# Low-rank decay columns computed with the first head's values and transposed, and the first weights in slots

## The chip, the core and the metric

The kernel runs on one core of one Trainium2 chip. The core has a matrix engine (PE in the profile, with PEld for its weight loads), three engines for element-wise work (DVE, ACT and POOL), and SP, on whose queue most transfers are issued. Each engine takes its instructions in the order in which the program gives them, and waits on semaphores for what the others have to finish first. The metric is the time of one execution on the device in microseconds (us); the median of several runs counts.

## The reference

One layer of a hybrid encoder on 1024 tokens of 1024 features, in fp32. What matters here is the normalised input, the one projection that feeds everything behind it, and the decay that is made of 32 of its columns:

```python
h = rmsnorm(x, norm_mix[l])
proj = h @ w_in[l]
q, k, v, r, lr_f, lr_b, u, g_a, g_b = jnp.split(proj, split_points, axis=-1)
log_a_f = jax.nn.log_sigmoid((lr_f @ w_decay_up_fwd[l] + b_decay_fwd[l]).astype(jnp.float32)) / GATE_NORMALIZER
log_a_b = jax.nn.log_sigmoid((lr_b @ w_decay_up_bwd[l] + b_decay_bwd[l]).astype(jnp.float32)) / GATE_NORMALIZER
...
```

`lr_f` and `lr_b` have 16 columns each: the low-rank columns. `q` and `k` have 4 heads of 128 columns, `v` 4 heads of 256. Behind it come gated linear attention in both directions, a pooling mixer, their merge, an output projection and a feed-forward network.

## The kernel before

**Numbers.** PE multiplies in fp32r. Each operand is split into a high part (ACT casts it) and a low part (DVE or POOL subtracts the high part from the source; `split_to`, L196 to L198), and a product is three matmuls: high by high, high by low, low by high (`mm3`). Names ending in h and l are such pairs: `hh` and `hl` the normalised input, `wh` and `wl` weights, `vh` and `vl` values.

**The start.** SP's queue carries the first tiles of `x`, six small vectors into `rows` (gains and decay biases; `load_rows`, L353), the first head's V weights in four parts (`fetch`, L243), more tiles of `x`, and `lraw`, the 32 low-rank columns of `w_in` for all features. PE transposes `rows` into `vps`, DVE copies it to `cols`. A tile is 128 tokens. For each, ACT makes the mean square, DVE and POOL the factor `n1rs`, DVE scales to `xn` (`norm_x`); PE transposes `xn` so that features lie on partitions (`tr`); ACT and DVE apply the gain and split it into `hh` and `hl` (`gain_and_split`, L320 to L330).

**The value tiles.** The loop over the eight tiles, numbered 0 to 7, in pairs (L428 to L443) makes the first head's values (`values`, L380): in each tile eight feature blocks by three matmuls, with 128 tokens of `hh` or `hl` stationary and 256 weight columns moving, into one PSUM bank, and then the split into `vh` and `vl`. Beside it runs a generator that `pump` advances after each feature block by credits: in even tiles (until tile 2) the norms of later tiles, in odd tiles up to 5 a block of four transposes after feature blocks 0, 2, 4 and 6, with their `gain_and_split`, for the next two tiles. Each tile's products can start once the features of its pair are split.

**The low-rank stage.** `low_rank_weights` (L396) casts `lraw` to `lw`, with the 32 columns repeated four times, three times the high part and once the low part. After the loop (L445 to L456), for each half of the tokens 16 matmuls with `lw` stationary and 512 tokens of `hh` or `hl` moving give the low-rank columns with features on partitions (128 rows: four copies of 32); `lrT` is their cast, with one group of rows replaced by the residual. Products with `up`, made of the two small decay matrices, use it later, after the projections of Q and K.

**Weights.** The class `Weights` (L213) takes tiles from rings of buffers; their casts and subtractions are steps in `pending`, which `pump` takes up one by one. `fetch` loads the next weights of the list `order`, `prepare` puts their splitting up, `take` waits for it. For the first weights DVE subtracts in part 0 and POOL in parts 1 to 3.

**Order.** The program's order is that of each engine. Eight semaphores are handed round among the DMAs; a DMA that takes one again waits until the transfer that had it before has landed.

Of the kernel before, what the change touches and what calls it, by code (L numbers as in the profile page):

```python
# [10 lines left out]
F32 = mybir.dt.float32  # L11
F32R = mybir.dt.float32r
# [3 lines left out]
ALU = mybir.AluOpType  # L16

P = 128
D = 1024
SEQ = 1024  # L20
KT = D // P
NT = SEQ // P
HALF = 512
HEADS = 4
DK = 128
DV = 256
RANK = 16
# [8 lines left out]
Q0, K0, V0, R0 = 0, 512, 1024, 2048  # L36
LR0 = 3072
U0 = LR0 + 2 * RANK
# [4 lines left out]
AHEAD = 4  # L43
PUT = 3
POOLING = 1.75

SLOTS = 39
MM_BANKS = 3
# [3 lines left out]
def kernel(  # L52
# [20 lines left out]
    nc = tc.nc  # L73
    x, out = x[0], out[0]
    w_in, w_branch, w_out = w_in[0], w_branch_gla[0], w_out[0]
# [4 lines left out]
    wts = ctx.enter_context(tc.tile_pool(name="wts", bufs=6))  # L80
    tmp = ctx.enter_context(tc.tile_pool(name="tmp", bufs=5))
    small = ctx.enter_context(tc.tile_pool(name="small", bufs=5))
    ps_mm = ctx.enter_context(tc.tile_pool(name="ps_mm", bufs=MM_BANKS, space=bass.MemoryType.PSUM))
    ps_g = ctx.enter_context(tc.tile_pool(name="ps_g", bufs=8 - MM_BANKS, space=bass.MemoryType.PSUM))
# [6 lines left out]
    def name(s):  # L91
        count[0] += 1
        return f"{s}_{count[0]}"

    def slot(dtype=F32, shape=(2, HALF), s="slot"):
        return slots.tile([P, *shape], dtype, tag="slot", name=name(s))
# [4 lines left out]
    def s1(shape=(256,), s="s"):  # L101
        return small.tile([P, *shape], F32, tag="s1", name=name(s))
# [4 lines left out]
    def bank(pool, s="ps"):  # L107
        return pool.tile([P, HALF], F32, tag=pool.name, name=name(s))

    def as_f32(ap):  # L110
        return ap.bitcast(F32)


    ident = const.tile([P, P], F32, tag="ident", name="ident")
# [36 lines left out]
    def soon(delay, *steps):  # L151
        put_off.extend([delay, step] for step in steps)
# [5 lines left out]
    def pump(dt):  # L158
        for entry in put_off:
            entry[0] -= dt  # L160
        while put_off and put_off[0][0] <= 0:
            put_off.pop(0)[1]()
        if pending:
            credit[0] += dt
            if credit[0] >= 2:
                credit[0] = 0.0
                pending.pop(0)()
        if aside:
            aside[0][1] -= dt

            if aside[0][1] <= 0 and not pending:
                cost = next(aside[0][0], None)
                if cost is None:
                    aside.pop(0)
                else:
                    aside[0][1] += cost
        if not side:
            return
        side[0][1] -= dt
        while side and side[0][1] <= 0:  # L180
            try:
                side[0][1] += next(side[0][0])
            except StopIteration:
                side.pop(0)

    def begin(gen, delay=0.0):
        side.append([gen, delay])

    def finish_side():
        while side:  # L190
            for _ in side[0][0]:
                pass
            side.pop(0)


    def split_to(hi, lo, src, eng=nc.vector):  # L196
        nc.scalar.copy(hi, src)  # L197
        eng.tensor_tensor(lo, src, as_f32(hi), op=ALU.subtract)  # L198
# [13 lines left out]
    class Weights:  # L212
# [8 lines left out]
        def split(self, raw):  # L221
            hi = wts.tile(list(raw.shape), F32R, tag="wh", name=name("wh"))[:, :, :]
            lo = wts.tile(list(raw.shape), F32R, tag="wl", name=name("wl"))[:, :, :]
            split_to(hi, lo, raw[:, :, :], nc.gpsimd if hT.tiles else nc.vector)
            self.parts.append((hi, lo))

        def finish(self):
# [3 lines left out]
        def __call__(self, k):  # L231
            return tuple(t[:, k % self.per, :] for t in self.parts[k // self.per])


    order = []
    for h in range(HEADS):
        cols_of = [(Q0 + h * DK, DK), (K0 + h * DK, DK), (V0 + h * DV, DV)]
        order += [(w_in, KT, *c) for c in (cols_of if h else cols_of[2:] + cols_of[:2])]
    order += [(w_in, KT, R0 + j * P, P) for j in range(KT)]
    order = iter(order)  # L240
    loaded, ready = [], []

    def fetch():  # L243
        src = next(order, None)
        if src is not None:
            loaded.append(load(*src))

    def prepare():
        if not loaded:
            fetch()  # L250
        if loaded:
            ready.append(Weights(loaded.pop(0)))

            credit[0] = -2.0

    def take(ahead=True):

        if not ready:
            prepare()
        w = ready.pop(0)  # L260
        w.finish()
        if ahead:
            prepare()
        return w
# [3 lines left out]
    def products(ps, a, b, first=True, last=True, onto=False):  # L268

        for n, (i, j) in enumerate(((0, 0), (0, 1), (1, 0))):  # L270
            nc.tensor.matmul(ps, a[i], b[j], start=first and n == 0, stop=last and n == 2, skip_group_check=onto)  # L271

    def mm3(ps, a, b, first, last, onto=False):
        products(ps, a, b, first, last, onto)
        pump(ps.shape[-1] / HALF)
# [15 lines left out]
    def tokens(pair, t):  # L291
        return tuple(p[:, (t % 4) * P : (t % 4 + 1) * P] for p in pair)
# [52 lines left out]
    n_rows = sum(n for _, n in vec_rows)  # L345
    rows = tmp.tile([n_rows, P], F32, tag="t2", name="rows")
    uraw = slot(F32, (HEADS, 2, DK), "uraw")
    lraw = slot(F32, (KT, 2 * RANK), "lraw")

    def load_x(t):  # L350
        nc.sync.dma_start(xt[t % 4][:, :], x[t * P : (t + 1) * P, :])

    def load_rows(at, v, n):  # L353
        nc.sync.dma_start(rows[at : at + n, :], v[0].rearrange("(j p) -> j p", p=P))

    def load_up(i, d, w):
        r = 2 * RANK * i + RANK * d
        nc.sync.dma_start(uraw[r : r + RANK, :, d, :], w[0].rearrange("r (h c) -> r h c", h=HEADS))

    load_x(0)  # L360
    load_rows(0, *vec_rows[0])
    load_x(1)
    for i in range(1, len(vec_rows)):
        load_rows(sum(n for _, n in vec_rows[:i]), *vec_rows[i])
    fetch()
    for t in (2, 3):
        load_x(t)
    nc.sync.dma_start(lraw[:, :, :], w_in[:, LR0:U0].rearrange("(k p) c -> p k c", p=P))
    nc.gpsimd.memset(uraw[:, :, :, :], 0.0)

    hT = Activations("h")
# [12 lines left out]
    def values(w, v, t):  # L384
        ps = bank(ps_mm)
        for kt in range(KT):
            mm3(ps[:, :DV], tokens(hT(kt, t // 4), t), w(kt), kt == 0, kt == KT - 1)
        split_to(*(part[:, t % 4, :] for part in v[t // 4]), ps[:, :DV])
# [1 line left out]

    lw = [wts.tile([P, 4, 4, 2 * RANK], F32R, tag="wh", name=name("lw")) for _ in range(2)]
    up = slot(F32R, (HEADS, 2, DK), "up")

    def low_rank_weights():  # L396
        for i in range(2):
            raw = lraw[:, 4 * i : 4 * i + 4, :]
            nc.scalar.copy(lw[i][:, :, :3, :], raw.unsqueeze(2).broadcast_to([P, 4, 3, 2 * RANK]))
            nc.vector.tensor_tensor(lw[i][:, :, 3, :], raw, as_f32(lw[i][:, :, 0, :]), op=ALU.subtract)  # L400
        nc.scalar.copy(up[:, :, :, :], uraw[:, :, :, :])
        nc.vector.tensor_tensor(up[32:64], uraw[32:64], as_f32(up[32:64]), op=ALU.subtract)

    def value_slots():
        return [(slot(F32R, (4, DV), "vh"), slot(F32R, (4, DV), "vl")) for _ in range(2)]

    v = value_slots()
# [10 lines left out]
    for t in range(2):  # L418
        for kp, ps in enumerate(trs):
            transpose_tile(ps, xn[t], t, kp)  # L420
    prepare()
    for kp, ps in enumerate(trs):
        pending.pop(0)()
        gain_and_split(ps, kp, 0, hT, g_mix)
    w = take(ahead=False)
    norm_x(2)
    norm_x(3)
    for t in range(0, NT, 2):  # L428
        if t + 4 < NT:
            begin(norms(t + 4), 1)  # L430
        if t == 2:
            for d, w_up in enumerate((w_decay_up_fwd, w_decay_up_bwd)):
                for i in range(4):
                    load_up(i, d, w_up)
        values(w, v, t)
        finish_side()
        if t + 2 < NT:
            begin(to_features(xn[(t + 2) % 4 :], t + 2, hT, g_mix), 0.5)
        values(w, v, t + 1)
        finish_side()  # L440
        if t == 4:
            low_rank_weights()
    prepare()  # L443
    lrT = slot(F32R, (2, HALF), "lrT")
    for half in range(2):  # L445
        ps = bank(ps_mm)
        for k in range(KT):
            for i in range(2):
                nc.tensor.matmul(
                    ps[:, :], lw[k // 4][:, k % 4, :, :].rearrange("p a r -> p (a r)"), hT(k, half)[i],  # L450
                    start=k == 0 and i == 0, stop=k == KT - 1 and i == 1,
                )
            pump(2 / 3)
        nc.scalar.copy(lrT[:, half, :], ps[:, :])
        nc.vector.tensor_tensor(lrT[64:96, half, :], ps[64:96, :], as_f32(lrT[64:96, half, :]), op=ALU.subtract)


    deferred = []

    def later(dst, src):  # L460
# [376 lines left out]
    for h in range(HEADS):  # L837
# [4 lines left out]
        if h > 0:  # L842
            v = value_slots()
            w = take()
# [136 lines left out]
    for j in range(KT):  # L981
# [6 lines left out]
        w = take()  # L988
# [7 lines left out]
        for half in range(2):  # L996
            ps = feature_major(w, hT, half)
# [188 lines left out]
    def pooling():  # L1186

        for g in range(GROUPS):
# [7 lines left out]
            for cost in pooled(g, u, hi, lo):  # L1196
                yield POOLING * cost
            yield 4
# [646 lines left out]
```

## Time and profile before

| | |
|---|---|
| median of 3 runs | 1407.31 us (1405.72 to 1408.82) |
| span of the profiled execution | 1405.0 us |
| instructions in the span | 18577 |
| value tiles, first to last matmul on PE | 10.77 to 43.57 us |
| low-rank stage on PE | 43.41 to 50.69 us |

The profile is one execution, recorded by the hardware. The span runs from its first to its last instruction; the device time also holds what lies around it. In rows of the timeline the first number is the start from the beginning of the span, the second the duration, both in us; then come the engine, the line of the program, the operation, what it writes and reads with shapes, how many instructions the row holds and, in brackets, how long the engine was idle before it and who ended that. Matmuls are pipelined: the distance of two starts is what one costs in a stream, and the duration of one is longer. Rows of stages have the length of the stage, the busy time and count for each engine, the clock granted to PE (1.00 is full speed), the DMA share and GB/s.

### The profile page before, as it was taken

To read this page: it belongs to the slowest core of one execution; us is meant where nothing else is said; L and a number is where in the kernel's file an instruction comes from. 1 tells how busy PE (TensorE), PEld (TensorE's weight loads), DVE (VectorE), ACT (ScalarE), POOL (GpSimd) and SP (SyncE) were. 2 spreads that over 40 slices of the span, in tenths; PEclk is the share of its full clock that TensorE was granted. 3 is DMA by queue.
4 is the path that set the end of the run, shared out by engine and by line. 5 is a ranking of instruction groups with operands and counts; after the bars stand their busy time and mean duration, and the time that the engine had idled before them with its cause. 6 is when DMAs were issued, how large, how long until landed. Compare 5 with 4: busy or idle time off the path is not lost.

```text
span 1405.0 us, 18577 instructions
## 1 busy us (share of the span) xinstructions
PE 1372.1 (98%) x6677; PEld 1155.0 (82%) x6677; DVE 842.7 (60%) x1073; ACT 623.5 (44%) x1119; POOL 751.0 (53%) x558
## 2 busy tenths in 40 slices
PE   7999999999999989999999999999999999999997
PEld 6889898988888768788887788888888888888876
DVE  6266757567745666677885865555655556343363
ACT  6364655554333444455356633333333334443253
POOL 3251616141288446567666076667666667464354
PEclk9999999999999999999999999999999999999999
DMA  6212413322377558998524555554444447976451
GB/s 192 76 46 61 135 52 114 98 69 75 121 214 250 195 173 273 334 406 291 185 75 151 186 188 173 173 167 148 140 146 148 140 155 255 387 259 222 165 227 72
DMA packets 167612, 243.62 MB, mean 173 GB/s; under 512 B 10936, under 2 KB 98016, under 8 KB 167520
## 3 DMA queue, kind: packets, MB, share of 16 engines
q1 hardware_dynamic: 167520, 242.45, 51.0%
q8 instruction: 52, 0.85, 0.2%
q14 instruction: 40, 0.33, 0.1%
HBM read 164.55 MB, written 77.86 MB: 173 GB/s over the span
## 4 chain that ended last, share of the span: by engine, by line
PE 67%; DVE 5%; issue 3%; DMA 2%; POOL 2%; ACT 2%; SPq 0%; POOLq 0%; ACTq 0%; DVEq 0%
PE ps L271 64%; DMA fraw<-in_w_in_dram 1%; POOL wl L198 1%; PE yb L271 1%; PE tp L959 0%; DMA gor<-g_out 0%; DMA wor<-t_out 0%; DVE fs L869 0%; PE op L800 0%; DVE ws L1033 0%; POOL fraw L600 0%; DVE x L1523 0%; POOL mg L1150 0%; DMA u_out<-uph 0%; ACT wh L197 0%
## 5 line engine op out<-in xcount | busy, mean ns | idle before, releaser
L198 POOL TENSOR_TENSOR wl<-fs,wh 128x512 fp32r<-128x512 f32 x120 | 166.1, 1388 | 172.1 <-ACT wh L197 138.6
L271 PE MATMUL ps<-gl,wh 128*128 128x512 f32 x616 | 239.8, 389 | 0.9 <-DVE gl L1439 0.9
L271 PE MATMUL ps<-gh,wh 128*128 128x512 f32 x616 | 240.3, 390 | 0.0
L271 PE MATMUL ps<-gh,wl 128*128 128x512 f32 x616 | 239.7, 389 | 0.0
L198 POOL TENSOR_TENSOR wl<-fraw,wh 128x512 fp32r<-128x512 f32 x90 | 128.9, 1432 | 60.1 <-ACT wh L197 57.3
L198 POOL TENSOR_TENSOR ol<-gor,oh 128x1024 fp32r<-128x1024 f32 (+1 forms) x42 | 100.1, 2389 | 93.2 <-ACT oh L197 87.5
L271 PE MATMUL ps<-hh,wh 128*128 128x512 f32 x376 | 149.6, 398 | 0.0
L271 PE MATMUL ps<-hh,wl 128*128 128x512 f32 x376 | 147.0, 391 | 0.0
L271 PE MATMUL ps<-hl,wh 128*128 128x512 f32 x376 | 146.7, 390 | 0.0
L198 POOL TENSOR_TENSOR wl<-raw,wh 128x512 fp32r<-128x512 f32 x47 | 64.5, 1389 | 146.6 <-ACT wh L197 135.7
L271 PEld LDWEIGHTS ps<-gl,wh 128*128 128x128 f32 x616 | 115.6, 188 | 25.0 <-DVE gl L1439 1.3
L271 PEld LDWEIGHTS ps<-gh,wl 128*128 128x128 f32 x616 | 115.6, 188 | 23.9
L271 PEld LDWEIGHTS ps<-gh,wh 128*128 128x128 f32 x616 | 115.6, 188 | 23.9
L271 PE MATMUL ps<-oh,oh 128*128 128x512 f32 x308 | 119.9, 389 | 1.1 <-DVE x L1767 1.1
L271 PE MATMUL ps<-ol,oh 128*128 128x512 f32 x308 | 119.9, 389 | 0.2 <-DVE ol L198 0.2
L271 PE MATMUL ps<-oh,ol 128*128 128x512 f32 x308 | 119.8, 389 | 0.0
L198 POOL TENSOR_TENSOR wl<-wraw,wh 128x512 fp32r<-128x512 f32 x56 | 89.8, 1631 | 45.1 <-ACT wh L197 45.0
L198 DVE TENSOR_TENSOR ol<-wor,oh 128x1024 fp32r<-128x1024 f32 (+1 forms) x42 | 62.0, 1496 | 54.0 <-ACT oh L197 46.7
L197 ACT CAST wh<-fs 128x512 fp32r<-128x512 f32 x120 | 73.7, 614 | 29.0 <-DVE fs L869 27.8
L271 PEld LDWEIGHTS ps<-hh,wl 128*128 128x128 f32 x376 | 70.7, 188 | 15.1
L271 PEld LDWEIGHTS ps<-hl,wh 128*128 128x128 f32 x376 | 70.9, 188 | 13.6
L271 PEld LDWEIGHTS ps<-hh,wh 128*128 128x128 f32 x376 | 70.8, 188 | 13.5
(251 smaller groups left out, 3183.0 us busy)
## 6 DMA issues: line engine op xcount, KB each, us to landing
fraw<-in_w_ffn_in_dram SPq DMA_DIRECT2D x44, 512.0 KB, 5.9
gor<-g_out SPq DMA_DIRECT2D x35, 512.0 KB, 6.1
raw<-in_w_in_dram SPq DMA_DIRECT2D x48, 256.0 KB, 3.2
g_out<-s SPq DMA_DIRECT2D x44, 256.0 KB, 2.3
fraw<-in_w_in_dram SPq DMA_DIRECT2D x20, 512.0 KB, 6.8
wor<-t_out SPq DMA_DIRECT2D x20, 512.0 KB
g_out<-g SPq DMA_DIRECT2D x33, 256.0 KB, 2.6
x<-in_x_dram SPq DMA_DIRECT2D x16, 512.0 KB, 5.7
```

The costliest lines, as they stand in the source:

```text
L197: nc.scalar.copy(hi, src)
L198: eng.tensor_tensor(lo, src, as_f32(hi), op=ALU.subtract)
L271: nc.tensor.matmul(ps, a[i], b[j], start=first and n == 0, stop=last and n == 2, skip_group_check=onto)
```

## The change

The 32 low-rank columns of `w_in` stand behind the 256 columns of the first head's V weights in the same tiles, so that a value matmul has 288 moving columns (`VL`). In the bank of each value tile, columns 256 to 287 then hold the low-rank columns with tokens on partitions. ACT copies them, repeated four times, to `lr` (128 x 128); PE transposes `lr` into the bank `lt`, in the next tile's matmuls after feature block 1, and for tile 7 within Q's first ones. After four of them ACT casts the bank to `lrT` and DVE makes the residual rows. The low-rank stage, `lw` and `lraw` go.

The first weights have slots of their own. Their narrow columns are loaded on ACT's queue ahead of all else, their wide ones on SP's. The split goes to DVE in parts 0 and 2 and to POOL in parts 1 and 3. Three instead of four copies of each decay matrix are loaded to `uraw`. Q's weights are fetched in the loop and put up for splitting within it.

```diff
+VL = DV + 2 * RANK
...
-            split_to(hi, lo, raw[:, :, :], nc.gpsimd if hT.tiles else nc.vector)
+            split_to(hi, lo, raw[:, :, :], nc.gpsimd)
...
+    class FirstWeights(Weights):
+        def split(self, raw):
+            hi, lo = (slot(F32R, (2, VL), s) for s in ("fwh", "fwl"))
+            split_to(hi[:, :, :], lo[:, :, :], raw[:, :, :], nc.gpsimd if len(self.parts) % 2 else nc.vector)
+            self.parts.append((hi, lo))
+
+    def load_first():
+        tiles = [slot(F32, (2, VL), "fraw") for _ in range(KT // 2)]
+        for i, t in enumerate(tiles):
+            rows_in = slice(2 * i * P, (2 * i + 2) * P)
+            nc.scalar.dma_start(t[:, :, DV:], w_in[rows_in, LR0:U0].rearrange("(k p) c -> p k c", p=P))
+        return tiles
+
+    def load_first_values(tiles):
+        for i, t in enumerate(tiles):
+            rows_in = slice(2 * i * P, (2 * i + 2) * P)
+            nc.sync.dma_start(t[:, :, :DV], w_in[rows_in, V0 : V0 + DV].rearrange("(k p) c -> p k c", p=P))
...
-        order += [(w_in, KT, *c) for c in (cols_of if h else cols_of[2:] + cols_of[:2])]
+        order += [(w_in, KT, *c) for c in (cols_of if h else cols_of[:2])]
...
+    first_raw = load_first()
     load_x(0)
...
-    fetch()
+    load_first_values(first_raw)
     for t in (2, 3):
         load_x(t)
-    nc.sync.dma_start(lraw[:, :, :], w_in[:, LR0:U0].rearrange("(k p) c -> p k c", p=P))
...
+    def up_weights():
         nc.scalar.copy(up[:, :, :, :], uraw[:, :, :, :])
         nc.vector.tensor_tensor(up[32:64], uraw[32:64], as_f32(up[32:64]), op=ALU.subtract)
+
+    low_rows, low_banks = {}, {}
+
+    def first_values(w, v, t):
+        ps = bank(ps_mm)
+        for kt in range(KT):
+            mm3(ps[:, :VL], tokens(hT(kt, t // 4), t), w(kt), kt == 0, kt == KT - 1)
+            if kt == 1 and t - 1 in low_rows:
+                transpose_low(t - 1)
+        split_to(*(part[:, t % 4, :] for part in v[t // 4]), ps[:, :DV])
+        low_rows[t] = s1((4, 2 * RANK), "lr")
+        nc.scalar.copy(low_rows[t][:, :, :], ps[:, DV:VL].unsqueeze(1).broadcast_to([P, 4, 2 * RANK]))
+
+    def transpose_low(t):
+        half, i = t // 4, t % 4
+        if i == 0:
+            low_banks[half] = bank(ps_g, "lt")
+        ps = low_banks[half]
+        nc.tensor.transpose(
+            ps[:, i * P : (i + 1) * P], low_rows.pop(t).rearrange("p a r -> p (a r)"), ident[:, :]
+        )
+        if i == 3:
+            nc.scalar.copy(lrT[:, half, :], ps[:, :])
+            nc.vector.tensor_tensor(lrT[64:96, half, :], ps[64:96, :], as_f32(lrT[64:96, half, :]), op=ALU.subtract)
...
-    prepare()
+    w = FirstWeights(first_raw)
...
-                for i in range(4):
+                for i in range(3):
                     load_up(i, d, w_up)
-        values(w, v, t)
+        first_values(w, v, t)
...
-        values(w, v, t + 1)
+        first_values(w, v, t + 1)
         finish_side()
+        if t == 2:
+            fetch()
         if t == 4:
-            low_rank_weights()
-    prepare()
-    lrT = slot(F32R, (2, HALF), "lrT")
-    for half in range(2):
-        ps = bank(ps_mm)
-        for k in range(KT):
-            for i in range(2):
-                nc.tensor.matmul(
-                    ps[:, :], lw[k // 4][:, k % 4, :, :].rearrange("p a r -> p (a r)"), hT(k, half)[i],
-                    start=k == 0 and i == 0, stop=k == KT - 1 and i == 1,
-                )
-            pump(2 / 3)
...
+            up_weights()
+            prepare()
+    soon(1, partial(transpose_low, NT - 1))
```

The next rows are ACT's order around the end of value tile 0, before and then with the change. `ps_256` and `ps_257` are the bank of tile 0, `tr_299` and `tr_302` the first block of transposes for tiles 2 and 3; the names in brackets are the engines whose semaphores are waited for.

```order
L311 ACTIVATE xn_131,n1ms_281<-x_127 128x1024 [waits DMAHW0_49,DVE_49]
L197 CAST vh_160<-ps_256 128x256 [waits PE_49]
L325 ACTIVATE hh_206<-tr_299,cols 128x256 [waits PE_49]
L325 ACTIVATE hh_206<-tr_299,cols 128x256
L325 ACTIVATE hh_216<-tr_314,cols 128x256 [waits PE_49]
```

```order
L331 ACTIVATE xn_131,n1ms_282<-x_127 128x1024 [waits DMAHW3_49,DVE_49]
L198 CAST vh_161<-ps_257 128x256 [waits PE_49]
L430 COPY lr_296<-ps_257 128x128 [waits DVE_49]
L345 ACTIVATE hh_207<-tr_302,cols 128x256 [waits PE_49]
L345 ACTIVATE hh_207<-tr_302,cols 128x256
L345 ACTIVATE hh_217<-tr_319,cols 128x256 [waits PE_49]
```

A copy to `lr` now stands between the cast of the values and the casts of the features, and it waits for DVE: for the count that DVE reaches with `vl` of the same tile.

On PE the rows are those of tile 1 with the change, from the end of the block of transposes that follows its feature block 0 to the start of feature block 2. `ps_298` is the bank of tile 1, `lt_314` the bank for the transposed low-rank columns.

```order
L338 MATMUL tr_302<-ident,xn_133 128x128 [waits DVE_49]
L338 MATMUL tr_302<-ident,xn_133 128x128
L291 MATMUL ps_298<-fwh_203,hh_207 128x288
L291 MATMUL ps_298<-fwl_204,hh_207 128x288
L291 MATMUL ps_298<-fwh_203,hl_208 128x288
L438 MATMUL lt_314<-ident,lr_296 128x128 [waits PE_49,Activation_49]
L291 MATMUL ps_298<-fwh_213,hh_217 128x288
```

The transpose of tile 0's copy stands within tile 1 and waits for ACT.

On SP the rows are the first loads of the program, before and then with the change.

```order
L351 DMA x_127<-in_x_dram 128x1024
L354 DMA rows<-in_norm_ffn_dram 8x128
L354 DMA rows<-in_gla_norm_dram 8x128
L354 DMA rows<-in_pool_scale_dram 8x128
L354 DMA rows<-in_b_decay_fwd_dram 4x128
L354 DMA rows<-in_b_decay_bwd_dram 4x128
L205 DMA raw_145<-in_w_in_dram 128x2x256 [waits DMAHW0_49]
```

```order
L370 DMA x_127<-in_x_dram 128x1024
L373 DMA rows<-in_norm_ffn_dram 8x128
L373 DMA rows<-in_gla_norm_dram 8x128 [waits DMAHW0_49]
L373 DMA rows<-in_pool_scale_dram 8x128 [waits DMAHW1_49]
L373 DMA rows<-in_b_decay_fwd_dram 4x128 [waits DMAHW2_49]
L373 DMA rows<-in_b_decay_bwd_dram 4x128 [waits DMAHW3_49]
L253 DMA fraw_136<-in_w_in_dram 128x2x256 [waits DMAHW4_49]
```

The four narrow loads on ACT's queue hold the first four semaphores, so the last four loads of `rows` wait for them to land.

More of the change, by code (lines that the diff above doesn't have):

```diff
@@ L347 @@
     uraw = slot(F32, (HEADS, 2, DK), "uraw")
-    lraw = slot(F32, (KT, 2 * RANK), "lraw")
     def load_x(t):
@@ L388, in values @@
         split_to(*(part[:, t % 4, :] for part in v[t // 4]), ps[:, :DV])
-    lw = [wts.tile([P, 4, 4, 2 * RANK], F32R, tag="wh", name=name("lw")) for _ in range(2)]
     up = slot(F32R, (HEADS, 2, DK), "up")
-    def low_rank_weights():
-        for i in range(2):
-            raw = lraw[:, 4 * i : 4 * i + 4, :]
-            nc.scalar.copy(lw[i][:, :, :3, :], raw.unsqueeze(2).broadcast_to([P, 4, 3, 2 * RANK]))
-            nc.vector.tensor_tensor(lw[i][:, :, 3, :], raw, as_f32(lw[i][:, :, 0, :]), op=ALU.subtract)
+    lrT = slot(F32R, (2, HALF), "lrT")
+    def up_weights():
         nc.scalar.copy(up[:, :, :, :], uraw[:, :, :, :])
         nc.vector.tensor_tensor(up[32:64], uraw[32:64], as_f32(up[32:64]), op=ALU.subtract)
+    low_rows, low_banks = {}, {}
[19 more added lines that the diff above has]
+            nc.vector.tensor_tensor(lrT[64:96, half, :], ps[64:96, :], as_f32(lrT[64:96, half, :]), op=ALU.subtract)
     def value_slots():
@@ L424 @@
         gain_and_split(ps, kp, 0, hT, g_mix)
-    w = take(ahead=False)
+    w.finish()
     norm_x(2)
@@ L438 @@
             begin(to_features(xn[(t + 2) % 4 :], t + 2, hT, g_mix), 0.5)
-        values(w, v, t + 1)
+        first_values(w, v, t + 1)
         finish_side()
+        if t == 2:
+            fetch()
         if t == 4:
-            low_rank_weights()
-    prepare()
-    lrT = slot(F32R, (2, HALF), "lrT")
-    for half in range(2):
-        ps = bank(ps_mm)
-        for k in range(KT):
-            for i in range(2):
-                nc.tensor.matmul(
-                    ps[:, :], lw[k // 4][:, k % 4, :, :].rearrange("p a r -> p (a r)"), hT(k, half)[i],
-                    start=k == 0 and i == 0, stop=k == KT - 1 and i == 1,
-                )
-            pump(2 / 3)
-        nc.scalar.copy(lrT[:, half, :], ps[:, :])
-        nc.vector.tensor_tensor(lrT[64:96, half, :], ps[64:96, :], as_f32(lrT[64:96, half, :]), op=ALU.subtract)
+            up_weights()
+            prepare()
+    soon(1, partial(transpose_low, NT - 1))
     deferred = []
```

## The prediction

> **What bounds the kernel now.** I read the page from the top: the span, the busy times, and the chain of work that ended last.
>
> ```profile
> span 1405.0 us, 18577 instructions
> PE 1372.1 (98%) x6677; PEld 1155.0 (82%) x6677; DVE 842.7 (60%) x1073; ACT 623.5 (44%) x1119; POOL 751.0 (53%) x558
> PE 67%; DVE 5%; issue 3%; DMA 2%; POOL 2%; ACT 2%; SPq 0%; POOLq 0%; ACTq 0%; DVEq 0%
> ```
>
> PE is busy for 98% of the span and carries the chain. An instruction taken from PE is therefore time won where PE has no idle time, and a wait put into PE's stream is time lost there. So I asked for busy time by stage. The columns are the stage, its length, the busy time of PE, weight load, DVE, ACT and POOL, then the granted clock.
>
> ```profile
> 0.00:75.00 75.00, 65.19 (x397) 58.11 (x398) 30.79 (x71) 36.72 (x77) 18.94 (x54) 1.00 0.42 125
> 29.50:43.00 13.50, 13.50 (x117) 13.50 (x116) 9.02 (x22) 7.46 (x18) 0.00 (x0) 1.00 0.07 19
> ```
>
> The change lies within the first 75 us. There PE is idle for 9.8 us, nearly all of it before 29.5, and from 29.5 to 43, the later value tiles, it is idle for nothing: there is no slack in that stretch to hide a new wait. Behind the change the order on every engine is as before, so what the first 50 us win or lose is handed on to the end by a busy PE.
>
> **Removed: the low-rank stage.** The timeline of PE at its two ends:
>
> ```profile
> 43.29 0.28 PE L271 MATMUL ps<-wh,hl 128*128 128x256 f32 x1
> 43.41 0.40 PE L449 MATMUL ps<-hh,lw 128*128 128x512 f32 x1
> ...
> 50.69 0.39 PE L271 MATMUL ps<-hh,wh 128*128 128x512 f32 x1
> ```
>
> 32 matmuls start from 43.41 on and the first projection of Q starts at 50.69, 0.2275 each without a gap: **-7.28 us**, all of it on the path.
>
> **Added: 32 columns.** Eight tiles of 24 matmuls are 192. From 43.29 to 43.41 a matmul of 256 columns takes 0.12 us, one of 512 takes 0.2275. The slope is 0.1075 us per 256 columns, 0.0134 for 32, so that one takes 0.133: 192 x 0.0134 = **+2.58 us**.
>
> **Added: eight transposes on PE.** No single one stands in a stream of matmuls before, but blocks of four do:
>
> ```profile
> 33.30 0.29 PE L271 MATMUL ps<-wh,hl 128*128 128x256 f32 x1
> 33.43 0.60 PE L318 MATMUL tr<-ident,xn 128*128 128x128 f32 x4
> 33.78 0.36 PE L271 MATMUL ps<-wh,hh 128*128 128x256 f32 x1
> 33.98 0.28 PE L271 MATMUL ps<-wl,hh 128*128 128x256 f32 x1
> ```
>
> From 33.30 to 33.98 pass 0.68 us where two matmuls alone take 0.24: a block costs 0.44. Of this the four need 0.35 (33.43 to 33.78), 0.088 each, and the rest, 0.08, is the slower matmul behind them. One alone costs 0.17: 8 x 0.17 = **+1.36 us**. Up to here the sum is -3.34.
>
> **Added: the wait at each transpose.** PE takes its work in order, so the transpose of tile t, which stands behind the second feature block of tile t+1, holds everything behind it until ACT's copy `lr` of tile t is there. And by the built program this copy waits for DVE's `vl` of the same tile: the two read the same PSUM bank and are put in sequence. So the chain behind a value tile is: ACT's `vh`, DVE's `vl`, ACT's `lr`, PE. ACT takes work in order too: behind the waiting copy are the casts of `hh` and the squares for the norms. The copy itself is not in the trace; casts on ACT take 0.37 us at 256 columns and 0.62 at 512 (rows below), about 0.98 ns per column, so I take 0.25 for 128; at the 0.37 of 256 columns all eight waits below would grow by 0.12, 1.0 in all, and at the 0.19 of DVE's copy of 40 columns (a row further down) shrink by 0.5. Between dependent engines pass about 0.04 us (43.57, where the last matmul ends, to 43.61 here):
>
> ```profile
> 43.61 0.37 ACT L197 CAST vh<-ps 128x256 fp32r<-128x256 f32 x1 [2.51 <-PE ps L271]
> 43.88 0.62 ACT L197 CAST wh<-raw 128x512 fp32r<-128x512 f32 x1
> 44.01 0.42 DVE L198 TENSOR_TENSOR vl<-ps,vh 128x256 fp32r<-128x256 f32 x1 [1.94 <-ACT vh L197]
> ```
>
> This is the chain with both engines idle: `vl` ends at 44.43, the copy at 44.72, the transpose may start at 44.76. With six matmuls of 0.133 from 43.41 PE would be there at 44.21: **0.55** late, the stall in tile 7. At Q three wide matmuls (0.68) come first: 44.09, so **0.65**. In tile 5 a block of transposes (0.44) comes first too: **0.1**.
>
> Where DVE is busy it is later. In tiles 2, 4 and 6 the casts of the transposes of the tile before stand ahead of `vl`; the rows are those of tile 6:
>
> ```profile
> 36.87 0.60 PE L318 MATMUL tr<-ident,xn 128*128 128x128 f32 x4
> 37.22 0.36 PE L271 MATMUL ps<-wh,hh 128*128 128x256 f32 x1
> 38.23 0.37 ACT L197 CAST vh<-ps 128x256 fp32r<-128x256 f32 x1
> 38.38 0.88 DVE L328 SCALAR_TENSOR_TENSOR hl<-tr,cols,hh 128x256 fp32r<-128x256 f32 x2 [0.27 <-ACT hh L325]
> 39.17 0.41 DVE L198 TENSOR_TENSOR vl<-ps,vh 128x256 fp32r<-128x256 f32 x1
> ```
>
> `vl` ends at 39.58, the transpose may start at 39.91; PE is there nine matmuls after 37.22, at 38.5: 1.4 late, three times **4.2**.
>
> In tile 1 DVE holds two norms ahead of `vl`:
>
> ```profile
> 18.64 0.44 PE L318 MATMUL tr<-ident,xn 128*128 128x128 f32 x2 [1.04 <-DVE n1rs L302]
> 18.83 0.36 PE L271 MATMUL ps<-wh,hh 128*128 128x256 f32 x1
> 19.37 0.35 ACT L197 CAST vh<-ps 128x256 fp32r<-128x256 f32 x1
> 21.45 0.42 DVE L198 TENSOR_TENSOR vl<-ps,vh 128x256 fp32r<-128x256 f32 x1
> ```
>
> `vl` ends at 21.87, the transpose may start at 22.2; PE is there at 19.3, three matmuls after 18.83: **2.9**. In tile 3 the norms of tile 2 stand ahead:
>
> ```profile
> 23.55 1.08 ACT L311 ACTIVATE xn<-x 128x1024 f32<-128x1024 f32 x1
> 25.25 0.14 DVE L302 TENSOR_SCALAR n1rs<-n1ms 128x1 f32<-128x1 f32 x1
> 28.34 0.42 DVE L198 TENSOR_TENSOR vl<-ps,vh 128x256 fp32r<-128x256 f32 x1
> ```
>
> Counted from the end of the copy that freed tile 2: the square takes 1.2 with its read-out, the chain from `n1rs` to the end of `vl` 3.5 (25.25 to 28.76), the copy 0.3, together 5.0. PE needs 18 matmuls (2.4), six more (0.8), a block and a transpose: 3.85. Late by **1.15**. All waits: 0.55 + 0.65 + 0.1 + 4.2 + 2.9 + 1.15 = **+9.55 us**. The low bound is 2.25: had the copy to wait for `vh` alone, tile 1 would be 0.75 late, tiles 2, 4, 6 0.4 each, the last two 0.3.
>
> The Trainium skill, "PSUM — Partial Sum Buffer", section "PSUM bank collisions raise a hardware error", states that two engines on one bank and quadrant at once are an error, reads against reads included; it speaks against a change that gives a bank a second reader on another engine. By that rule the sum is the one with 9.55 and not the one with 2.25; no run here shows a collision.
>
> **Moved: the start.** Four narrow loads (128-byte runs) now go out on ACT's queue first, and eight semaphores are handed round, so the last four loads of `rows` on SP each wait for a narrow load to land.
>
> ```profile
> 0.80 0.39 SPq L351 DMA_DIRECT2D x<-in_x_dram  x1
> 3.44 0.29 SPq L354 DMA_DIRECT2D rows<-in_b_decay_bwd_dram  x1
> 6.71 0.30 PE L411 MATMUL vps<-ident,rows 40*128 40x40 f32 x1 [6.71 <-DMA rows<-in_b_decay_bwd_dram]
> 7.13 0.19 DVE L413 COPY cols<-vps 128x40 f32<-128x40 f32 x1
> 7.52 0.15 DVE L302 TENSOR_SCALAR n1rs<-n1ms 128x1 f32<-128x1 f32 x1 [0.20 <-ACT xn L311]
> DMA to landing us min/median/max: 2.1/2.7/3.3
> DMA to landing us min/median/max: 2.8/3.1/3.7
> ```
>
> The last two are the landings of `uraw` (16 partitions) and `raw` (256 KB). Issues 0.4 apart put the fourth at 2.0; at `uraw`'s 2.7 it lands at 4.7, and the last `rows` goes out then, not at 3.44: 1.26 later. DVE's copy of the columns has 0.2 to spare ahead of the second tile's `n1rs`, which starts the next tile's way to PE: 1.0 late. With landings of 2.1 and 3.7 it is 0.4 and 2.1; I take 1.0, near `uraw`, the smaller load, and bounds of 0 and 2.1. Three wider casts of the first weights on ACT add 0.06 each: **+1.2 us**.
>
> **At nothing.** The first weights' residual moves from POOL to DVE for one of four:
>
> ```profile
> PE ps L271 <- POOL wl L198: 1.0, 3, 0.5
> ```
>
> PE waits 1.0 for POOL there, but ahead of the norms for which it waits 1.04 at 18.64 anyhow. The earlier fetch and casts of Q's weights lie under tiles 3 to 7, and ACT is busy for 7.46 of 13.5 us there. The casts of `lrT` are needed by the decay products only after Q's and K's projections. Without that cover they would cost about one cast each, 0.6.
>
> **Sum.** -7.28 + 2.58 + 1.36 + 9.55 + 1.2 = **+7.4 us**: from the profiled span of 1405.0 to 1412.4, and from the median of 1407.31, which holds 2.3 us around the span, to **1414.7**.
>
> **The rivals.** B, half clock. After an idle of 2.27 us PE ran slow later in the program:
>
> ```profile
> 514.72 0.50 PE L271 MATMUL ps<-trh,wh 128*128 128x512 f32 x1 [2.27 <-DVE ga L1237]
> 515.00:520.00 5.00, 5.00 (x16) 3.95 (x16) 4.90 (x6) 2.28 (x5) 3.05 (x2) 0.66 0.00 0
> 517.15 0.63 PE L271 MATMUL ps<-trh,wl 128*128 128x512 f32 x1
> 517.58 0.63 PE L271 MATMUL ps<-trh,wh 128*128 128x512 f32 x1
> ```
>
> The granted clock is 0.66 over 515 to 520, and matmuls start 0.43 apart: 5 x 0.34 = 1.7 us lost. The stall of 2.9 in tile 1 is longer, with 1.04 of idle just ahead of it at 18.64. Once gives 1416.4, twice 1418.1. Against it: one idle is one case. The Trainium skill, "TensorE: Matmul & The Clock Gate", section "Part 1: The HAM clock gate", puts the throttle behind an idle window of about 3.4 us; by that rule 2.9 would cost nothing more, but the trace shows half clock after 2.27, and the measurement decides.
>
> C, the copy does not wait for `vl` on the chip, or DVE gets there earlier than its rows say: stalls of 2.25, so -3.34 + 2.25 + 1.2 = +0.1, 1407.4. The order of waits in the built program speaks against it.
>
> D, faster: the copy of each tile lands within the 0.8 us that PE needs for six matmuls, and the start does not move. Then -3.34 stands alone, 1404.0; it decides as soon as stalls and start together stay under 0.5. Against it, `vh`, `vl` and copy are 1.04 even with idle engines.
>
> **Chances.** The forecast 0.55 (1413.2 to 1416.8 with the bounds of the start and of the copy), B 0.27, C 0.10, D 0.04, several costs beyond these 0.04. Within 0.2%, 2.8 us, is about what a measurement of this kernel can tell from no change: 1404.5 to 1410.1. So faster 0.05, same 0.09, slower 0.86. The range takes in the forecast and B: 1410.5 to 1419.5.
>
> **What would show it.** PE from the last value tile straight to Q, with no 512-column low-rank matmuls; value matmuls 0.133 apart; in PE's waits eight at the new transpose, for ACT's copy, near 2.9, 1.4, 1.15, 1.4, 0.1, 1.4, 0.55 and 0.65, and on ACT the copy idle for DVE's `vl`; the start of the columns' copy near 8.4 instead of 7.13; a clock under 1.00 around 22 to 26 for B. I am wrong if the copies run right behind `vh`, or if the stalls move what comes later.

## The result and the profile after

The changed kernel takes 1415.17 us (median of 4 runs, 1414.63 to 1417.15), the kernel before beside it 1407.18. The medians are 8.0 us apart, where +7.4 was forecast. The ratio over all runs, which need not be the quotient of the medians, is 1.0062 (95% interval 1.0050 to 1.0075): slower. Measured a second time (experiment 5), the medians were 10.5 us apart and the ratio 1.0070 (1.0057 to 1.0082).

The page of the changed kernel, in the rows that answer to those of before: span, busy times, and shares of the chain that ended last.

```profile
span 1415.4 us, 18528 instructions
PE 1372.9 (97%) x6653; PEld 1154.9 (82%) x6653; DVE 844.6 (60%) x1072; ACT 624.8 (44%) x1125; POOL 750.0 (53%) x557
PE 60%; DVE 6%; issue 4%; POOL 4%; DMA 3%; ACT 2%; SPq 0%; POOLq 0%; DVEq 0%; ACTq 0%
```

The span is 10.4 us longer than before, and PE is busy for 0.8 us more: the loss is idle time of PE. This profiled execution is the slowest of the four, which matters below. What PE waited for up to 80 us, with the sum, the count and the longest:

```profile
PE vps L452 <- DMA rows<-in_b_decay_bwd_dram: 8.6, 1, 8.6
PE lt L438 <- ACT lr L430: 8.4, 7, 2.7
PE tr L338 <- DVE n1rs L322: 1.6, 2, 1.0
PE ps L291 <- POOL fwl L199: 1.1, 2, 0.6
```

The second row is new: the eight transposes, seven of them waiting for ACT's copy. Who holds the copy is seen on ACT and DVE in tile 1, and what it does to PE on PE's own timeline:

```profile
20.43 0.35 ACT L198 CAST vh<-ps 128x256 fp32r<-128x256 f32 x1
23.60 0.27 ACT L430 COPY lr<-ps 128x128 f32<-128x128 f32 x1 [2.82 <-DVE vl L199]
23.15 0.42 DVE L199 TENSOR_TENSOR vl<-ps,vh 128x256 fp32r<-128x256 f32 x1
20.88 0.29 PE L291 MATMUL ps<-fwh,hl 128*128 128x288 f32 x1
23.92 0.48 PE L438 MATMUL lt<-ident,lr 128*128 128x128 f32 x1 [2.75 <-ACT lr L430]
```

The copy is done as soon as `vl` is, and not sooner, 3.2 us after the cast of the same bank began. PE could have gone on at 20.88 + 0.133 = 21.01 and did so at 23.92: 2.91. The profile calls 2.75 of this idle, because a matmul's row lasts longer than its share of the stream; by distances of starts each wait is 0.16 longer than its idle time. The other waits, and the matmuls around the one in tile 2:

```profile
30.13 0.30 PE L291 MATMUL ps<-fwl,hh 128*128 128x288 f32 x1
...
30.92 0.29 PE L291 MATMUL ps<-fwl,hh 128*128 128x288 f32 x1
31.06 0.29 PE L291 MATMUL ps<-fwh,hl 128*128 128x288 f32 x1
32.63 0.33 PE L438 MATMUL lt<-ident,lr 128*128 128x128 f32 x1 [1.28 <-ACT lr L430]
32.71 0.38 PE L291 MATMUL ps<-fwh,hh 128*128 128x288 f32 x1
32.92 0.29 PE L291 MATMUL ps<-fwl,hh 128*128 128x288 f32 x1
...
37.52 0.33 PE L438 MATMUL lt<-ident,lr 128*128 128x128 f32 x1 [0.93 <-ACT lr L430]
...
43.62 0.33 PE L438 MATMUL lt<-ident,lr 128*128 128x128 f32 x1 [1.27 <-ACT lr L430]
...
53.72 0.33 PE L438 MATMUL lt<-ident,lr 128*128 128x128 f32 x1 [1.26 <-ACT lr L430]
...
57.66 0.33 PE L438 MATMUL lt<-ident,lr 128*128 128x128 f32 x1 [0.42 <-ACT lr L430]
...
61.59 0.33 PE L438 MATMUL lt<-ident,lr 128*128 128x128 f32 x1 [0.52 <-ACT lr L430]
61.67 0.47 PE L291 MATMUL ps<-hh,wh 128*128 128x512 f32 x1
```

With 0.16 added these are 1.44, 1.09, 1.43, 1.42, 0.58 and 0.68 for tiles 2, 3, 4, 6, 7 and Q; tile 5 waits 0.2 (its matmul ahead of the transpose starts at 47.28, the transpose at 47.61, where 0.13 is due). The sum is 9.75.

The start, by SP's, PE's and DVE's rows:

```profile
2.06 0.33 SPq L373 DMA_DIRECT2D rows<-in_norm_ffn_dram  x1
4.81 0.29 SPq L373 DMA_DIRECT2D rows<-in_gla_norm_dram  x1
...
6.93 0.29 SPq L373 DMA_DIRECT2D rows<-in_b_decay_bwd_dram  x1
8.62 0.30 PE L452 MATMUL vps<-ident,rows 40*128 40x40 f32 x1 [8.62 <-DMA rows<-in_b_decay_bwd_dram]
8.95 0.20 DVE L454 COPY cols<-vps 128x40 f32<-128x40 f32 x1 [1.52 <-PE vps L452]
...
20.34 0.44 PE L338 MATMUL tr<-ident,xn 128*128 128x128 f32 x2 [1.04 <-DVE n1rs L322]
```

SP stood from 2.4 to 4.81 ahead of the third load of `rows`, and the last went out at 6.93 where it was 3.44. The second pair of transposes for tiles 2 and 3 is 1.70 later than before (18.64). The clock, by stretches (the number behind the five engines):

```profile
20.00:23.00 3.00, 0.84 (x5) 0.60 (x5) 1.67 (x5) 0.78 (x3) 1.10 (x2) 0.96 0.87 246
23.00:26.00 3.00, 2.08 (x9) 2.07 (x10) 1.44 (x4) 1.00 (x3) 0.00 (x0) 0.50 0.58 168
26.00:29.00 3.00, 3.00 (x14) 2.98 (x14) 0.88 (x2) 1.54 (x4) 0.00 (x0) 0.50 0.82 197
29.00:32.00 3.00, 2.35 (x16) 2.10 (x15) 1.81 (x5) 1.24 (x4) 0.00 (x0) 0.90 0.55 157
```

PE ran at half clock until about 29.6. Windows of 0.25 us put the start of this stretch at 22.78, while PE still waited, and its end at 29.61: 6.83 us, of which 1.1 fell into the wait. From 23.92 to 29.91 it did one transpose, 15 matmuls and three blocks, which at full clock take 0.17 + 15 x 0.133 + 3 x 0.44 = 3.5; it took 6.0. That is 2.5 us, and it is what rival B was about.

### The profile page after: what moved, and what is told of

Same layout as the page of the kernel before. It is cut to its first block, busy times and chain, and to the rows that moved or that the text cites. A ratio compares the mean times of both kernels' runs of the same rounds, so it can differ in the third digit from the quotient of the medians.

```text
span 1415.4 us, 18528 instructions
## 1 busy us (share of the span) xinstructions
PE 1372.9 (97%) x6653; PEld 1154.9 (82%) x6653; DVE 844.6 (60%) x1072; ACT 624.8 (44%) x1125; POOL 750.0 (53%) x557
## 4 chain that ended last, share of the span: by engine, by line
PE 60%; DVE 6%; issue 4%; POOL 4%; DMA 3%; ACT 2%; SPq 0%; POOLq 0%; DVEq 0%; ACTq 0%
PE ps L291 58%; POOL wl L199 2%; DMA fraw<-in_w_in_dram 1%; DVE res L1768 1%; DMA pl<-p_out 1%; POOL wsum L630 1%; PE tp L989 0%; DMA wor<-t_out 0%; PE op L830 0%; DVE ws L1063 0%; DVE x L1553 0%; PE yb L291 0%; POOL n3rs L1536 0%; DVE ws L1055 0%; POOL mg L1180 0%
## 5 line engine op out<-in xcount | busy, mean ns | idle before, releaser
L199 POOL TENSOR_TENSOR wl<-raw,wh 128x512 fp32r<-128x512 f32 x44 | 61.0, 1400 | 145.3 <-ACT wh L198 145.3
```

## The experiments

Each is the changed kernel with an edit. Ratios are to the kernel before, run beside it on the same chip (its medians: 1406.4 for the first four, 1406.0 for the next four, 1405.72 for the last two).

**1. The copy first.**

```diff
-        split_to(*(part[:, t % 4, :] for part in v[t // 4]), ps[:, :DV])
         low_rows[t] = s1((4, 2 * RANK), "lr")
         nc.scalar.copy(low_rows[t][:, :, :], ps[:, DV:VL].unsqueeze(1).broadcast_to([P, 4, 2 * RANK]))
+        split_to(*(part[:, t % 4, :] for part in v[t // 4]), ps[:, :DV])
```

> The changed kernel with one edit: ACT copies the low-rank columns to lr before it casts the values to vh, so the copy no longer waits for DVE's vl. Theory W (the eight waits of PE at the new transposes, 9.8 us by the distances of starts, come from the copy's wait for vl): each transpose finds its copy there or waits below 0.2 us, the value tiles take 24 x 0.133 us, no half clock around 24 to 30 us, and the time is 7.3 removed, 2.6 and 1.4 added, 1.7 for the later start: about 1405.5, a ratio to before near 0.999 (0.9975 to 1.0005). Rival L (the stall is the length of the path from PE through ACT back to PE, whatever the order): waits near 1 us each stay, 1412 to 1415. Rival S (the norms and casts on ACT and DVE set the pace and PE waits somewhere else): the waits go from the new transposes to tr or ps, and the time stays above 1410.

Measured: 1403.77 us, ratio 0.9980 (0.9972 to 0.9989). PE waits for no copy any more; the whole list up to 80 us, then ACT, DVE and PE in tile 1:

```profile
PE vps L452 <- DMA rows<-in_b_decay_bwd_dram: 9.0, 1, 9.0
PE tr L338 <- DVE n1rs L322: 1.6, 2, 1.0
PE ps L291 <- POOL fwl L199: 0.9, 2, 0.5
20.54 0.29 ACT L429 COPY lr<-ps 128x128 f32<-128x128 f32 x1
20.68 0.42 ACT L198 CAST vh<-ps 128x256 fp32r<-128x256 f32 x1
23.53 0.42 DVE L199 TENSOR_TENSOR vl<-ps,vh 128x256 fp32r<-128x256 f32 x1
21.92 0.41 PE L438 MATMUL lt<-ident,lr 128*128 128x128 f32 x1
```

DVE's order is the same as in the changed kernel, and its `vl` of tile 0 comes at 23.53, as late as ever. So the order of two readers of one bank made all eight waits; rivals L and S fall. Half clock is gone from 24 to 30 us, as expected, but it did not go altogether: it came earlier (0.57 over 20 to 24 us), although no long wait is left. The ratio is 0.001 below the expected one, within its range.

**2. The transposes later.**

```diff
-            if kt == 1 and t - 1 in low_rows:
+            if kt == 6 and t - 1 in low_rows:
```

> The changed kernel with one edit: the transpose of the tile before stands behind feature block 6 of a value tile, not behind block 1; the copy still waits for vl, and ACT is held as long as before. Theory W: PE reaches the transpose 15 matmuls (2.0 us) and up to three blocks of transposes (1.3 us) later than now, so the waits of 1.4 and below are covered, and of the 2.9 in tile 1 nothing or little is left; only the one at Q (0.7) stays. About 1406 to 1407, a ratio of 0.999 to 1.0005. Rival H (what costs is that ACT is held behind the copy, so that the casts of the features come late): PE waits at the next tile's first products or at the transposes instead, 1 to 2 us at tiles 2, 4 and 6, and the time is 1409 to 1414.

Measured: 1405.96 us, ratio 0.9994 (0.9985 to 1.0003). ACT is held as before, and PE hardly waits; ACT in tile 1, and PE's waits for the copy:

```profile
23.60 0.27 ACT L430 COPY lr<-ps 128x128 f32<-128x128 f32 x1 [3.04 <-DVE vl L199]
23.76 3.03 ACT L345 ACTIVATE hh<-tr,cols 128x256 fp32r<-128x256 f32 x8
...
PE lt L438 <- ACT lr L430: 1.1, 2, 0.6
```

No wait for `hh` or `hl` took the place of the removed ones. Holding ACT for 3 us costs nothing when the casts of the features behind it have until the next tile; PE standing in front of its transpose is what cost. One wait more than expected stayed: beside Q's, one of 0.58 us in the value tiles, at 38.07. Rival H falls.

**3. The narrow loads behind the wide ones.**

```diff
-            nc.scalar.dma_start(t[:, :, DV:], w_in[rows_in, LR0:U0].rearrange("(k p) c -> p k c", p=P))
...
             nc.sync.dma_start(t[:, :, :DV], w_in[rows_in, V0 : V0 + DV].rearrange("(k p) c -> p k c", p=P))
+            nc.sync.dma_start(t[:, :, DV:], w_in[rows_in, LR0:U0].rearrange("(k p) c -> p k c", p=P))
```

> The changed kernel with one edit: the four narrow loads go out on SP's queue, each behind the wide load of the same part, not first on ACT's. Theory N (the start is 1.7 us later because the last four loads of rows wait for the narrow ones to land): the copy of the columns on DVE starts at about 7.1 and not 8.95, the first transposes of tile 2 wait to 17.2 and not 18.85, and the time falls by about 1.5, to about 1413.6, a ratio near 1.005; the stalls at the new transposes stay. Rival M (the start is later because of the bytes and the wider casts): the columns come early but the value tiles start as late as now, and the time stays within 0.5 of 1415.2. Rival P (the wide loads and x now go out later by the narrow ones' issue, up to 1.6 us): the norms of tiles 2 and 3 come later than now, 1416 to 1417.

Measured: 1412.38 us, ratio 1.0047 (1.0035 to 1.0059). The loads of `rows` go out as before, and what hangs on them comes as before:

```profile
2.41 0.30 SPq L370 DMA_DIRECT2D rows<-in_gla_norm_dram  x1
...
3.42 0.29 SPq L370 DMA_DIRECT2D rows<-in_b_decay_bwd_dram  x1
7.12 0.19 DVE L451 COPY cols<-vps 128x40 f32<-128x40 f32 x1
...
18.61 0.44 PE L335 MATMUL tr<-ident,xn 128*128 128x128 f32 x2 [1.04 <-DVE n1rs L319]
PE lt L435 <- ACT lr L427: 8.4, 7, 2.7
```

18.61 against 20.34, and 18.64 before the change: the whole 1.7 of the start was the wait for a semaphore that a narrow load held. The traces settle this; the ratio's interval overlaps that of the changed kernel (1.0050 to 1.0075). The bytes and the wider casts (M) and the later wide loads (P) cost nothing that is seen.

**4. PE kept busy in the wait.**

```diff
+            if kt == 1 and t == 1:
+                idle = bank(ps_g, "idle")
+                for _ in range(20):
+                    nc.tensor.matmul(idle[:, :VL], tokens(hT(0, 0), 0)[0], w(0)[0], start=True, stop=True)
             if kt == 1 and t - 1 in low_rows:
```

> The changed kernel with one addition: in tile 1, ahead of the transpose for which PE waits 2.9 us, PE does 20 matmuls of 288 columns into a bank that nobody reads (2.7 us). Theory K (the clock is halved from 23 to 29.9 us in the profiled run because PE stood idle for 2.75 us, and that costs 2.5 us on top of the wait, in the executions in which it comes): with PE busy the clock stays at 1.00 there, every run is near the lowest ones of the changed kernel, 1414 to 1415, and the highest is below 1415.5. Rival T (half clock has another cause, the load of the engines or the transfers): 0.50 appears there as before, with times up to 1417. Rival X (the extra matmuls are not hidden): 1416 to 1418 with the clock at 1.00.

Measured: 1413.33 us, ratio 1.0051 (1.0038 to 1.0064). The clock is full where it was half:

```profile
21.32 2.79 PE L429 MATMUL idle<-fwh,hh 128*128 128x288 f32 x20
24.23 0.33 PE L442 MATMUL lt<-ident,lr 128*128 128x128 f32 x1
...
24.00:30.00 6.00, 4.96 (x38) 4.61 (x37) 3.83 (x9) 3.70 (x10) 0.00 (x0) 1.00 0.71 190
```

Q's first matmul behind the last transpose starts at 59.39, in the changed kernel at 61.67. The matmuls add work and take 2.3 us off. The mean clocks of the executions agree, with 0.998 to 0.999 in four of five here and 0.994 to 0.996 in the changed kernel, but a mean over the program does not say where the clock was low. In all four traces with the empty wait of 2.75 us (the changed kernel and experiments 3, 5 and 8) the clock is half for 6.83 us around it; in the one trace in which the wait is filled it is full. So the long stretch of half clock goes with PE standing idle there. Experiment 1 shows that a shorter one can come without a long wait.

**5 to 8.** The changed kernel again; both edits of 1 and 3; these with the transposes in groups of four; and one part of the change undone.

> The changed kernel once more, unedited, beside kernels of the same chip. If the half clock in tile 1 comes in only some executions and costs up to 2.5 us there, the runs spread over 1412.5 to 1417 and their median is 0.5 to 2 us above that of the kernel with 20 extra matmuls in that wait (ratio 1.0051); if it costs nothing, the ratio is the same 1.0051.

Measured: 1416.47 us, ratio 1.0070 (1.0057 to 1.0082), clocks of 0.994 to 0.995 in all five. Against 1.0051 in experiment 4, measured on another chip, that is 0.0019, 2.7 us, and the two intervals overlap a little; the traces, with 2.3 to 2.5 in tile 1, carry the size. The whole difference is not all tile 1: the kept trace of experiment 5 also has half clock later, at 244 and 524 us, and that of experiment 4 has none.

> The changed kernel with two edits together: ACT copies to lr ahead of vh, and the narrow loads stand on SP's queue behind the wide ones. Theory (the two costs are independent: 9.8 us of waits at the transposes, 1.7 us of start): the sum of the two gains, 1.7 below the kernel with the first edit alone (1403.8), so about 1402.1, ratio 0.9968 (0.996 to 0.9978), and no wait at the new transposes. Rival (with the waits gone, PE runs into the norms and casts of the next tiles, which do not come earlier): no gain over 1403.8, ratio 0.998.

Measured: 1400.99 us, ratio 0.9966 (0.9954 to 0.9979). PE waits for no copy at the new transposes, and the two gains add, within the interval; the rival's 0.998 lies just outside it. In the traces Q's second block starts 1.2 us earlier than in experiment 1 (49.78, was 50.99), less than the 1.7 that was due.

```diff
+    def transpose_four(t0):
+        for t in range(t0, t0 + 4):
+            transpose_low(t)
...
-            if kt == 1 and t - 1 in low_rows:
-                transpose_low(t - 1)
+            if kt == 1 and t == 4:
+                transpose_four(0)
...
-    soon(1, partial(transpose_low, NT - 1))
+    soon(1, partial(transpose_four, 4))
```

> As the kernel with both edits, and the eight transposes in two groups of four, one in tile 4 and one in Q's first matmuls. Theory (a transpose alone costs 0.17 on PE, four together 0.44, because the slower matmul behind them comes once): 0.5 us less than with both edits, about 1401.6, ratio 0.9965, which this measurement can hardly tell; the distances of starts in the trace show 0.44 for each group. Rival (four copies that stay longer, or a longer hold of the bank, delay the casts): as with both edits or up to 0.5 above.

Measured: 1401.95 us, ratio 0.9965 (0.9952 to 0.9979): not to be told from experiment 6. PE's rows around the first group:

```profile
33.46 0.29 PE L288 MATMUL ps<-fwh,hl 128*128 128x288 f32 x1
33.59 0.60 PE L435 MATMUL lt<-ident,lr 128*128 128x128 f32 x4
33.95 0.38 PE L288 MATMUL ps<-fwh,hh 128*128 128x288 f32 x1
34.16 0.29 PE L288 MATMUL ps<-fwl,hh 128*128 128x288 f32 x1
```

From 33.46 to 34.16 pass 0.70, of which 0.27 are the matmuls: 0.43 for four.

```diff
-            split_to(hi[:, :, :], lo[:, :, :], raw[:, :, :], nc.gpsimd if len(self.parts) % 2 else nc.vector)
+            split_to(hi[:, :, :], lo[:, :, :], raw[:, :, :], nc.gpsimd if self.parts else nc.vector)
```

> The changed kernel with one part undone: the first weights' residual is made by POOL in parts 1 to 3, as in the kernel before, and by DVE in part 0 only. Theory (the split on two engines is worth nothing, since PE waits for the norms of tiles 2 and 3 right behind it): the transposes of tile 2 start within 0.3 us of 18.85 and the time stays within 0.5 of the changed kernel on this chip. Rival G (the split on two engines wins what PE waits for POOL, 1.0 us or more): 1 to 2 us slower than the changed kernel. Rival V (part 2 on DVE delays the casts of the features and the norms): 0.5 to 1 faster.

Measured: 1415.84 us, ratio 1.0067 (1.0054 to 1.0079), beside 1.0070 for the unedited one: the split on two engines is worth nothing here. The first transposes in tile 1 start at 19.01, against 18.89 in experiment 5.

**9 and 10.** The best kernel with matmuls in the two short waits ahead of tile 1, and the width alone.

```diff
...
             for i in range(2):
+                if idle and kp == 0:
+                    for _ in range(8 if i else 5):
+                        idle(spare)
                 transpose_tile(ps, xn[i], i, kp)
...
```

> The kernel with both edits and the transposes in two groups of four, and in tile 1 PE does 5 and 8 matmuls of 288 columns into a bank that nobody reads, ahead of the two transposes for which it waits 0.55 and 1.04 us. Theory K (short idle times close together bring half clock, also with no wait at the new transposes: the clock was 0.57 to 0.75 over 20 to 24 us in the kernels without these waits): the clock is 1.00 there, and the time is 0.8 to 1.5 below the kernel without the extra matmuls in the executions that had it, ratio 0.9955 to 0.9962. Rival A (the half clock there is left over from the start and has nothing to do with these waits): it stays, ratio 0.9965 or above.

Measured: 1400.37 us, ratio 0.9958 (0.9945 to 0.9970), the fastest of all. The clock is 1.00 from 16 to 40 us in the profiled execution, but the kernel of experiment 10, with the same short waits and nothing in them, has 1.00 there too in its own trace, and the interval overlaps that of experiment 7. Theory K is not settled by this.

> The changed kernel without the copies to lr and the eight transposes: the 32 columns are computed and not used, and lrT is set to zero, so the decay has its bias alone. Theory: what is left of the change is 7.28 removed, 2.58 for the wider matmuls and 1.7 for the start, and half clock at tile 1 in some executions, as in the kernel that copies to lr first (ratio 0.998), less 1.4 for the eight transposes: ratio 0.9970 (0.996 to 0.998). Rival (the transposes cost more than their 0.17 each, since they take ACT's and the bank's time too): 2.5 us or more below that kernel, ratio under 0.996. Value matmuls start 0.133 apart.

This kernel leaves out the decay's low-rank part, so its output is not that of the layer; it serves for its time alone. Measured: 1402.83 us, ratio 0.9975 (0.9964 to 0.9985), against 0.9980 with the transposes in experiment 1. The difference, 0.7 us, fits the 1.4 expected for the eight within the intervals, and the rival, with 2.5 us or more below experiment 1, was not seen. The traces are sharper. From the last matmul of feature block 3 in tile 1, behind all half clock in that tile, to Q's first matmul pass 25.30 us here (22.24 to 47.54) and 26.20 in experiment 1 (24.06 to 50.26): 0.90 for six transposes, 0.15 each.

## Why the prediction held

Term by term, with the profiled executions of before and after:

| term | predicted | in the trace |
|---|---|---|
| low-rank stage | -7.28 | gone; Q follows the last value tile |
| 32 columns on 192 matmuls | +2.58 | 0.133 apart (30.13 to 31.06 in seven steps): +2.5 |
| eight transposes | +1.36 | 0.16 each (32.63 to 32.92, less 0.13): +1.3 |
| waits at the transposes | +9.55 | +9.75 |
| start | +1.2 | +1.7 |
| half clock (rival B) | 0, or 1.7 | +2.5 |
| sum | +7.4 | +10.5; Q's second block starts 10.3 later (61.67, was 51.37), the span is 10.4 longer |

The sum answers to the profiled execution, the slowest of the first four. The second measurement, 10.5 us by the medians, agrees with it; the first, 8.0, lies 2.5 lower, and no trace of one of its faster executions is there to say why. That 8.0 came so near the forecast's 7.4 is in part luck: the forecast left out half clock.

**The waits** were the step on which everything hung, and each of the eight came out within 0.15 of what the rows of before gave for it: 2.91 for 2.9, 1.44, 1.43 and 1.42 for 1.4, 1.09 for 1.15, 0.2 for 0.1, 0.58 for 0.55, 0.68 for 0.65. The copy took 0.27 for 0.25. Experiments 1 and 2 take the waits away in two ways, so their cause is shown, and rival C is excluded: the copy does wait for `vl`.

**The start** was right in its mechanism and half a microsecond short (the copy of the columns at 8.95, where 8.4 was forecast), but this small miss is two larger ones that nearly cancel, which is luck. The fourth narrow load was given a landing at 4.7; by the row of the last `rows` load it had landed at about 6.9, 2.2 later. And this last load then took 1.7 us to release PE (6.93 to 8.62), where before it took 3.3 (3.44 to 6.71): 1.6 sooner. The prediction had carried that time over unchanged; why it was shorter stays open. Experiment 3 shows that this wait is all of the loss.

**Half clock** was put beside the forecast as a rival with 0.27, and it is what the changed kernel does in both of its kept traces and in those of experiments 3 and 8, which have the same wait; of the other executions there are only mean clocks (0.994 to 0.996), which fit it but do not say where the clock was low. So the forecast's own case, full clock, is the one that did not hold in full: without half clock in tile 1 the kernel measures 1.0051 (experiment 4), 6.9 us by the medians and 7.2 by the ratio, near the forecast's 7.4; with it 1.0062 and 1.0070. Of the old median of 1407.31 these are 1416.0 and 1417.2: nearer to rival B's 1416.4 than to 1414.7, and within the range. The step that fell short is the choice of B as a rival at 0.27 instead of a term of the sum, and its price: 2.5 for the 1.7 that one place of before had shown. That place had 3.41 us of half clock, tile 1 has 6.83, twice as much, less the part that fell into the wait.

**At nothing** stood the split on two engines, and experiment 8 shows it to be worth nothing. Fetching and casting Q's weights earlier left no wait of its own in the list.

**Faster** needed each copy to land within six matmuls. That was not so as the change was written, with `vl` ahead of the copy. With two lines exchanged and four loads moved the same idea gives 0.9966: -7.28 + 2.58 + 1.36 is -3.3, and 4.7 to 5 us less are measured, with an interval (3.0 to 6.5) that takes in 3.3. Whether there is more, and what it comes from, was not pinned down; half clock at other places differs between the profiled executions (of before at 232 and 516 us, in the changed kernel at 244 and 524 us, in experiment 4 nowhere), by up to 3 us.

## What to carry to other kernels

When two engines read one PSUM bank, look at which of the reads stands first in the program: the short read whose result PE waits for goes first, and the long one, whose result nobody needs soon, may wait. Put a transpose or another consumer where its source is sure to be there, since PE in order pays for the difference in full. Loads put ahead of all others take the first semaphores of a small ring, and whatever is eight places behind waits for them to land: here a load went out at 6.93 instead of 3.44 us, and PE lost 1.7.

## What the runs showed of the hardware

In the kept traces, of before, of the changed kernel and of all ten experiments, half clock on PE came in stretches of 3.41 us or of twice that, 6.83, except where the program ended within one. It was 6.83 around the wait of 2.75 us in tile 1 (the changed kernel, experiments 3, 5 and 8), where it began before the wait was over. It was 3.41 at the two places of the kernel before, near 233 and 516 us, and in tile 1 of experiments 1, 2, 6 and 7, whose longest wait there was 1.04 to 1.16 us. With the same short waits it did not come in the traces of experiments 4 and 10. What decides whether a stretch comes is not shown.

Filling a wait with matmuls that nobody needs was faster than waiting, by 2.3 us at Q's start. A transpose of 128 x 128 in fp32 between these matmuls cost 0.16 us alone (32.63 to 32.92, less 0.13) and 0.43 for four in a row (experiment 7).
